# A hybrid encoder layer on one core: GpSimd issues the transfers of the mixer weights' split, only small parts are kept in DRAM, and the last tile is computed by token halves

## The chip, the core and the metric

One core of a Trainium2 chip runs the whole kernel. TensorE (PE) multiplies, VectorE (DVE), ScalarE (ACT) and GpSimd (POOL) do elementwise work, and SyncE (SP) only issues transfers; POOL and ACT can issue them too. Each engine carries out its own instructions in a fixed order and waits at the first one whose inputs or buffers are not ready. The metric is the device time of one launch in microseconds (us).

## The reference

One encoder layer over 512 tokens of width 1024, in float32:

```python
x = x + 0.5 * swiglu(rms_norm(x, ffn1_norm), ffn1_w_gate, ffn1_w_up, ffn1_w_down)   # d_ff 2816
h = rms_norm(x, mix_norm)
proj = h @ w_in
o_a = gdn_mixer(qkv_a, z_a, a_a, b_a, ...)      # gated DeltaNet, 4 heads, two directions, chunks of 64
o_b = dilated_mixer(qkv_b, ...)                 # windowed attention, 8 heads, 3 dilations
x = x + concatenate([o_a, o_b]) @ w_out
x = x + 0.5 * swiglu(rms_norm(x, ffn2_norm), ffn2_w_gate, ffn2_w_up, ffn2_w_down)
x = rms_norm(x, final_norm)
```

## The kernel before

**Layout.** Activations lie with the width on the 128 partitions and all 512 tokens in a row, so x is eight tiles of 128x512. Each float32 product is made from parts: a matrix is split into a big part (hi, a cast to the fp32r format) and a small part (lo, the rest), and `mm3` (line 53 for its matmuls) multiplies hi by hi, hi by lo and lo by hi into one PSUM bank. One weight tile of 8 blocks of 128x128 therefore costs 24 matmuls of 512 columns.

**Stages.** FFN 1: 22 steps f with a gate tile (pg) and an up tile (pu) each, 44 tiles of 24 matmuls, then 8 output tiles (pd) of 66 matmuls. The mixer: projections, attention, DeltaNet and output projection, an order of work written out by hand. FFN 2: as FFN 1, its first gate and up tiles fed as the mixer's are. Then the last norm and the output.

**Weights of the FFNs.** `wload` fetches 512 KB into `wraw` (2 buffers, issued by SP, line 175), ACT casts it to `whi` (line 176), DVE subtracts and writes `wlo` (line 177). TensorE needs both.

**Weights of the mixer.** There are 76 half tiles of 256 KB. During FFN 1 `presplit` prepares them: SP loads `praw` (line 202, 3 buffers), ACT casts it to `phi` (line 205, 2 buffers), DVE subtracts in place (line 206), and `send` has SP store both parts to DRAM (lines 193 and 194, tiles `ws`). `share` deals these steps over FFN 1. In the mixer `wnext` loads both parts again, 512 KB in one transfer (`wsp`, line 216), four tiles of buffers, and no engine but TensorE touches them. The order of the instructions on each engine is fixed when the kernel is built, by a scheduler: where a `phi` stands ahead of a `whi` on ACT, the `whi` can't start before it.

**The norm.** `Norm` squares x on ACT and adds the squares (line 263) on POOL or, with `fast`, on DVE; a matmul with ones (pr) sums over partitions; `rsq` makes the reciprocal root R.

**The end.** The eighth output tile of FFN 2 is computed over all 512 tokens; its two halves are then added to x, squared, summed (pr), turned into R, and all eight output tiles y are multiplied by R on DVE and POOL (line 1237) and stored.

Of the kernel before, what the change touches and what calls it, by code (L numbers as in the profile page):

```python
# [10 lines left out]
F32 = mybir.dt.float32  # L11
# [5 lines left out]
P = 128  # L17
# [16 lines left out]
N_MASK = 768  # L34
LV0, LVG, SCG, ATG = 9.0, 0.625, 0.8, 0.55
GIN, VGO, VGV, PRG, NRG, VTG, VBG, OPG, OTG, FNG, SVG, SSD, SST, VTP, LVH = 9.5, 16.5, 4.0, 0.5, 6.0, 3.5, 3.5, 13.5, 0.75, 10.5, 0.75, 8.0, 0.6, 3.0, 1.3
AHEAD = 3
PRI = 0, 1, 2, 4, 3, 5
ORDER = "rs@1 pa@3 K0 ab gt@2 Q0 K1 bi Q1 pc@3 g0 K3 Q2 K2 g1 Z0 g2 Q3 g3 V0 Pa0 V1 Z3 V2 V3 v0 Pb0 Z2 Z1 Pb1 v1 Pa1 v3 Pa2 Pb2 v2 Pb3 Pa3 oa"

# [50 lines left out]
def encoder_layer(ctx, tc, xT, gu1, dn1, win, wab, wo1, wo2, gu2, dn2, cols, relb, masks, onehot, lnc, sel, out):  # L91
# [49 lines left out]
    ve.tensor_scalar(out=col[:, 0:C_CONV], in0=col[:, 0:C_CONV], scalar1=-0.5, scalar2=None, op0=ALU.mult)  # L141
    gp.memset(ones, 1.0)
    gp.memset(eps, EPS)
    ve.tensor_scalar(out=wqk[:, 0:1], in0=col[:, C_QN:C_QN + 1], scalar1=-0.0625, scalar2=None, op0=ALU.mult)
    ve.tensor_scalar(out=wqk[:, 1:2], in0=col[:, C_KN:C_KN + 1], scalar1=-0.5, scalar2=None, op0=ALU.mult)

# [18 lines left out]
    def wload(src, n, k, low=False, parts=1, then=None):  # L165
        w = n * k
        raw = WF["pool"].tile([P, 1024], F32, tag="raw", name="wraw", bufs=2)
        if low:
            hi, lo = (wp.tile([P, 1024], F32R, tag="w", name=nm, bufs=4) for nm in ("whi", "wlo"))
        else:  # L170
            hi, lo = (WF["pool"].tile([P, 1024], F32R, tag=nm, name=nm, bufs=2) for nm in ("whi", "wlo"))
        sv = src.rearrange("p a b -> p (a b)")
        for i in range(parts):
            s = slice(i * w // parts, (i + 1) * w // parts)
            act["lastf"] = sy.dma_start(out=raw[:, s], in_=sv[:, s])
            se.copy(hi[:, s], raw[:, s])  # L176
            ve.tensor_tensor(out=lo[:, s], in0=raw[:, s], in1=hi.bitcast(F32)[:, s], op=ALU.subtract)  # L177
            if then is not None:
                then(i)
        return (hi[:, :w].rearrange("p (a b) -> p a b", b=k),  # L180
                lo[:, :w].rearrange("p (a b) -> p a b", b=k))
# [3 lines left out]
            for i in range(2)]  # L185
    plan += [wo1[d, :, 4 * u:4 * u + 4] for d in range(4) for u in range(3)] + [wo2[d] for d in range(4)]
    plan += [gu2[0, j, :, 4 * u:4 * u + 4] for j in range(2) for u in range(2)]
    ws_d = [dr.tile([P, 2 * T], F32, name=f"ws{i}") for i in range(len(plan))]
    made, raws, unsent = [0], [], []

    def send():
        i, hi, lo = unsent.pop(0)
        sy.dma_start(out=ws_d[i][:, 0:T], in_=hi.bitcast(F32))
        sy.dma_start(out=ws_d[i][:, T:2 * T], in_=lo)

    def presplit():

        i = made[0]
        made[0] += 1
        for n in range(i if i == 0 else i + 1, min(i + 2, len(plan))):  # L200
            raws.append(tmp("xp", "praw", T + 4, bufs=3)[:, 0:T])
            sy.dma_start(out=raws[-1], in_=plan[n].rearrange("p a b -> p (a b)"))
        lo = raws.pop(0)
        hi = WF["pool"].tile([P, T], F32R, tag="phi", name="phi", bufs=2)
        se.copy(hi, lo)  # L205
        ve.tensor_tensor(out=lo.bitcast(F32R), in0=lo, in1=hi.bitcast(F32), op=ALU.subtract)  # L206
        if unsent:
            send()
        unsent.append((i, hi, lo))

    taken, ready = [0], []

    def wnext():
        while taken[0] < len(plan) and len(ready) <= AHEAD:
            t = wp.tile([P, 1024], F32, tag="w", name="wsp", bufs=4)
            sy.dma_start(out=t, in_=ws_d[taken[0]])
            taken[0] += 1
            ready.append([t[:, i * T:(i + 1) * T].bitcast(F32R).rearrange("p (a b) -> p a b", b=P) for i in range(2)])
        return ready.pop(0)

    def sub(o, a, b):
        ve.tensor_tensor(out=o, in0=a, in1=b.bitcast(F32), op=ALU.subtract)  # L222
# [61 lines left out]
    def ffn(gu, dn, norm, nxt, then=None, late=False, mid=None):  # L284
        with tc.tile_pool(name="wf", bufs=2, reuse_waits="tile") as wf, \
                tc.tile_pool(name="hp", bufs=1, reuse_waits="tile") as hp:
            WF["pool"] = wf
            hh = [hp.tile([P, T], F32R, name=f"hh{f}") for f in range(NF)]
            hl = [hp.tile([P, T], F32R, name=f"hl{f}") for f in range(NF)]
            wait = []  # L290
            for f in range(NF):
                pg, pu = palt("pg"), palt("pu")
                for j, pt in ((0, pg), (1, pu)):
                    if f == 0 and late:
                        for u in (0, 4):
                            wh, wl = wnext()
                            for k in range(u, u + 4):
                                mm3(pt, wh[:, k - u], wl[:, k - u], xh[k], xl[k], k == 0, k == NKT - 1)
                        continue
                    first = then if f == 0 and j == 0 else None  # L300
                    wh, wl = wload(gu[f, j], NKT, P, True, 4 if first else 2 if f == 0 else 1, first)
                    if not late:
                        share(2 * f + j)
                    for k in range(NKT):
                        mm3(pt, wh[:, k], wl[:, k], xh[k], xl[k], k == 0, k == NKT - 1)
                wait.append((f, pg, pu))
                if f == (0 if late else 1):
                    with tc.issue_after(norm.last.ins):
                        for k in range(NKT):
                            norm.sq(k)  # L310
                    norm.rstd()
                if f == 0 and not late:
                    continue
                for e, pg, pu in wait:
                    g, u = tmp("g", "g"), tmp("u", "u")
                    ve.tensor_tensor(out=g, in0=pg, in1=R, op=ALU.mult)
                    silu(g, g)
                    ve.tensor_tensor(out=u, in0=pu, in1=R, op=ALU.mult)
                    ve.tensor_tensor(out=u, in0=u, in1=g, op=ALU.mult)
                    split(hh[e], hl[e], u)  # L320
                wait = []
            for d in range(NKT):
                pd = palt("pd")
                for f0, n in ((0, 8), (8, 8), (16, 6)):
                    wh, wl = wload(dn[d, :, f0:f0 + n], n, P)
                    if not late:
                        share(2 * NF + 3 * d + f0 // 8)
                    for i in range(n):
                        f = f0 + i
                        mm3(pd, wh[:, i], wl[:, i], hh[f], hl[f], f == 0, f == NF - 1)  # L330
                    if late and d == NKT - 1 and f0 == 8:
                        with tc.issue_after(act["mm"].ins):
                            mid()
                for s in (slice(0, 256), slice(256, 512)) if late and d == NKT - 1 else (slice(0, 512),):
                    ve.scalar_tensor_tensor(out=x[d][:, s], in0=pd[:, s], scalar=0.5, in1=x[d][:, s], op0=ALU.mult,
                                            op1=ALU.add)
                nxt(d)

    n1 = Norm(C_F1, 7)

    def bring(i):
        for k in range(1 + 2 * i, min(3 + 2 * i, NKT)):
# [4 lines left out]
    ident = mk[:, M_ID:M_ID + P]  # L347

    vec_d = dr.tile([8, 1024], F32, name="vec_d")
    n2 = Norm(C_MIX, 7)  # L350
    x_d = dr.tile([NKT, P, T], F32, name="x_d")

    def after1(d):
# [6 lines left out]
    with tc.issue_after(act["lastf"].ins):  # L360
        sy.dma_start(out=mk, in_=masks)

    with ExitStack() as mctx:
        mp = mctx.enter_context(tc.tile_pool(name="mp", bufs=1, reuse_waits="tile"))

# [847 lines left out]
            ys.append(slot(f"xh{d}", "y"))  # L1213
            se.mul(ys[d], x[d], col[:, C_FIN + d:C_FIN + d + 1])

    def mid():
        for i, pr in enumerate(prs):
            te.matmul(pr[:, 0:256], lhsT=ones, rhs=n4.acc[:, 256 * i:256 * i + 256], start=True, stop=False)

    ffn(gu2, dn2, n3, last, late=True, mid=mid)  # L1220
    hs = [slice(256 * i, 256 * i + 256) for i in range(2)]
    tail = tmp("sq", "tail")
    preload()
    for pr, s in zip(prs, hs):
        se.activation(tail[:, s], x[7][:, s], AF.Square)
        te.matmul(pr[:, 0:256], lhsT=ones, rhs=tail[:, s], start=False, stop=True)
        rsq(R[:, s], pr[:, 0:256], 1024.0, "u")
    ys.append(slot("xh7", "y"))
    for d in range(NKT):
        y = ys[d]  # L1230
        if d == NKT - 1:
            ve.scalar_tensor_tensor(out=y, in0=x[d], scalar=col[:, C_FIN + d:C_FIN + d + 1], in1=R, op0=ALU.mult,
                                    op1=ALU.mult)
            (sy, se)[d % 2].dma_start(out=out[d], in_=y)
        else:
            for s in hs if d == 0 else (slice(0, T),):
                (gp if d in (1, 4) else ve).tensor_tensor(out=y[:, s], in0=y[:, s], in1=R[:, s], op=ALU.mult)  # L1237
                (sy, se)[d % 2].dma_start(out=out[d, :, s], in_=y[:, s])


def _bucket(rel):
# [77 lines left out]
```

## Time and profile before

| | |
|---|---|
| runs | 1119.83, 1121.74, 1124.93 us; median 1121.74 |
| profiled execution | 1124.95 us, span 1123.2 us |
| FFN 1 gate and up, FFN 1 output | 5.3 to 271.6, 271.6 to 396 us |
| mixer, FFN 2, end | 396 to 746, 746 to 1108, 1108 to 1123.2 us |
| busy share of the span | PE 95%, DVE 55%, ACT 39%, POOL 8% |

The profile comes from one profiled execution. Times in it are in us from the start of the span; the execution's own time is 1.75 us longer than the span. A matmul's recorded duration overlaps the next one's, so its cost is the spacing of starts.

### The profile page before, as it was taken

The page shows a single profiled execution, that of the slowest core. Times are in us where ns is not written, and L with a number is a line of the kernel's source. Part 1 is how long each engine was busy: PE and PEld are TensorE (multiplying, and loading weights), DVE is VectorE, ACT ScalarE, POOL GpSimd, SP SyncE. Part 2 cuts the span into 40 slices and gives each one's busy share as a digit, 9 for nine tenths or more (in the row PEclk, how much of TensorE's full clock was granted, in tenths as well). Part 3 has the DMA queues.
Part 4 walks back from the last instruction along what each step waited for, and adds up shares of the span by engine and source line. Part 5 has one row for each costly group of instructions (what it writes and reads, how often), then busy time and mean ns, then how long its engine had stood idle before and what let it go on. Part 6 is the DMA issues. An engine that isn't in the chain of part 4 may idle for free. (4 is left out here: it accounts for less than half of the span.)

```text
span 1123.2 us, 14359 instructions
## 1 busy us (share of the span) xinstructions
PE 1071.6 (95%) x5312; PEld 871.1 (78%) x5312; DVE 613.1 (55%) x1108; ACT 441.1 (39%) x812; POOL 90.3 (8%) x121
## 2 busy tenths in 40 slices
PE   8999999999999999999999989999999999999994
PEld 5787777777788868778788867778888888888883
DVE  5655655655443358678566778565444444522223
ACT  6533443444332226422574756344332222322221
POOL 3000000000011123440000020100000000001111
PEclk9999999999999999999999999999999999999997
DMA  7788888988993334676723363352222323323332
GB/s 258 263 267 281 278 290 285 297 279 278 305 306 120 99 117 158 188 229 217 181 86 99 112 212 111 110 191 93 95 94 94 97 97 107 96 86 101 100 88 75
DMA packets 85062, 191.99 MB, mean 171 GB/s; under 512 B 21520, under 2 KB 22320, under 8 KB 84992
## 3 DMA queue, kind: packets, MB, share of 16 engines
q1 hardware_dynamic: 80800, 178.68, 49.7%
q0 software_dynamic: 2896, 10.25, 3.0%
q10 hardware_dynamic: 1296, 2.15, 0.5%
q8 instruction: 41, 0.67, 0.3%
q14 instruction: 29, 0.24, 0.1%
HBM read 142.24 MB, written 48.81 MB: 170 GB/s over the span
## 5 line engine op out<-in xcount | busy, mean ns | idle before, releaser
L176 ACT CAST whi<-wraw 128x1024 fp32r<-128x1024 f32 (+1 forms) x138 | 137.5, 998 | 269.0 <-PE pd L53 91.3
L177 DVE TENSOR_TENSOR wlo<-wraw,whi 128x1024 fp32r<-128x1024 f32 (+1 forms) x138 | 159.9, 1159 | 107.4 <-ACT whi L176 105.2
L53 PE MATMUL pg<-xh,whi 128*128 128x512 f32 x344 | 136.8, 398 | 7.2 <-ACT whi L176 7.2
L53 PE MATMUL pg<-xh,wlo 128*128 128x512 f32 x344 | 136.5, 397 | 6.9 <-DVE wlo L177 6.9
L53 PE MATMUL pd<-hh,whi 128*128 128x512 f32 x352 | 137.9, 392 | 2.6 <-ACT whi L176 2.6
L53 PE MATMUL pu<-xh,wlo 128*128 128x512 f32 x344 | 134.8, 392 | 4.8 <-DVE wlo L177 4.8
L53 PE MATMUL pd<-hh,wlo 128*128 128x512 f32 x352 | 137.7, 391 | 0.0
L53 PE MATMUL pd<-hl,whi 128*128 128x512 f32 x352 | 137.5, 391 | 0.0
L53 PE MATMUL pg<-xl,whi 128*128 128x512 f32 x344 | 135.9, 395 | 0.1
L53 PE MATMUL pu<-xh,whi 128*128 128x512 f32 x344 | 134.1, 390 | 0.0
L53 PE MATMUL pu<-xl,whi 128*128 128x512 f32 x344 | 133.9, 389 | 0.0
L206 DVE TENSOR_TENSOR praw<-praw,phi 128x512 fp32r<-128x512 f32 x76 | 53.4, 706 | 116.1 <-ACT phi L205 116.0
L205 ACT CAST phi<-praw 128x512 fp32r<-128x512 f32 x76 | 47.0, 620 | 155.7 <-DMA praw<-in_win 103.3
L53 PEld LDWEIGHTS pg<-xh,wlo 128*128 128x128 f32 x344 | 65.3, 190 | 24.8 <-DVE wlo L177 11.3
L53 PEld LDWEIGHTS pg<-xh,whi 128*128 128x128 f32 x344 | 65.3, 190 | 22.5 <-ACT whi L176 8.7
L53 PEld LDWEIGHTS pu<-xh,wlo 128*128 128x128 f32 x344 | 64.5, 188 | 21.5 <-DVE wlo L177 8.4
L53 PEld LDWEIGHTS pd<-hh,whi 128*128 128x128 f32 x352 | 66.5, 189 | 16.7 <-ACT whi L176 3.1
L53 PEld LDWEIGHTS pd<-hh,wlo 128*128 128x128 f32 x352 | 66.3, 188 | 14.7 <-DVE wlo L177 0.9
L53 PEld LDWEIGHTS pg<-xl,whi 128*128 128x128 f32 x344 | 65.1, 189 | 16.1 <-DVE xl L269 2.5
L53 PEld LDWEIGHTS pd<-hl,whi 128*128 128x128 f32 x352 | 66.5, 189 | 14.0
L53 PEld LDWEIGHTS pu<-xl,whi 128*128 128x128 f32 x344 | 64.6, 188 | 13.5
L53 PEld LDWEIGHTS pu<-xh,whi 128*128 128x128 f32 x344 | 64.6, 188 | 13.5 <-ACT whi L176 0.3
(292 smaller groups left out, 1626.9 us busy)
## 6 DMA issues: line engine op xcount, KB each, us to landing
wraw<-in_gu SPq DMA_DIRECT2D x84, 512.0 KB, 3.9
wsp<-ws SPq DMA_DIRECT2D x76, 512.0 KB, 3.5
ws<-phi SPq DMA_DIRECT2D x76, 256.0 KB, 3.6
ws<-praw SPq DMA_DIRECT2D x76, 256.0 KB, 4.5
wraw<-in_dn SPq DMA_DIRECT2D x32, 512.0 KB, 3.6
praw<-in_win SPq DMA_DIRECT2D x56, 256.0 KB, 4.2
wraw<-in_dn SPq DMA_DIRECT2D x16, 384.0 KB, 3.2
praw<-in_wo SPq DMA_DIRECT2D x16, 256.0 KB, 4.1
```

What stands on the lines that cost most here:

```text
L53: self.last = f(*a, **k)
L176: se.copy(hi[:, s], raw[:, s])
L177: ve.tensor_tensor(out=lo[:, s], in0=raw[:, s], in1=hi.bitcast(F32)[:, s], op=ALU.subtract)
L205: se.copy(hi, lo)
L206: ve.tensor_tensor(out=lo.bitcast(F32R), in0=lo, in1=hi.bitcast(F32), op=ALU.subtract)
```

## The change

Four edits. First, POOL issues the loads and the stores of `presplit`, with four buffers of `praw` and loads two half tiles ahead; only the small part is stored. In the mixer, SP loads the small part (256 KB) and the raw weight (256 KB, into `wrw`, a tile cut in two halves), and ACT casts the big part from it (`wsp<-wrw`); three tiles of buffers hold hi and lo, the fourth is `wrw`. Second, the norms of FFN 1 and of the mixer add their squares on DVE. Third, the last output tile is computed for tokens 0 to 255 and then for 256 to 511, and the norm, the products with R and the stores of the first half are placed after the first matmuls of the second. Fourth, eight matmuls of ones by ones stand at the start.

```diff
+    pw = pat("warm")
+    for i in range(8):
+        te.matmul(pw[:, 0:P], lhsT=ones, rhs=ones, start=True, stop=True)
...
-            hi, lo = (wp.tile([P, 1024], F32R, tag="w", name=nm, bufs=4) for nm in ("whi", "wlo"))
+            hi, lo = (wtile(nm) for nm in ("whi", "wlo"))
...
     def send():
-        i, hi, lo = unsent.pop(0)
-        sy.dma_start(out=ws_d[i][:, 0:T], in_=hi.bitcast(F32))
-        sy.dma_start(out=ws_d[i][:, T:2 * T], in_=lo)
+        i, lo = unsent.pop(0)
+        gp.dma_start(out=ws_d[i], in_=lo)
     def presplit():
         i = made[0]
         made[0] += 1
-        for n in range(i if i == 0 else i + 1, min(i + 2, len(plan))):
-            raws.append(tmp("xp", "praw", T + 4, bufs=3)[:, 0:T])
-            sy.dma_start(out=raws[-1], in_=plan[n].rearrange("p a b -> p (a b)"))
+        if unsent:
+            send()
+        for n in range(0 if i == 0 else i + 2, min(i + 3, len(plan))):
+            raws.append(tmp("xp", "praw", T + 4, bufs=3)[:, 0:T] if n % 4 else
+                        WF["pool"].tile([P, T], F32, tag="praw", name="praw", bufs=1))
+            gp.dma_start(out=raws[-1], in_=plan[n].rearrange("p a b -> p (a b)"))
         lo = raws.pop(0)
-        hi = WF["pool"].tile([P, T], F32R, tag="phi", name="phi", bufs=2)
+        hi = WF["pool"].tile([P, T], F32R, tag="phi", name="phi", bufs=1)
         se.copy(hi, lo)
         ve.tensor_tensor(out=lo.bitcast(F32R), in0=lo, in1=hi.bitcast(F32), op=ALU.subtract)
-        if unsent:
-            send()
-        unsent.append((i, hi, lo))
-
-    taken, ready = [0], []
+        unsent.append((i, lo))
...
+    def wtile(name, dt=F32R):
+        nw[0] += 1
+        t, n = ("wb", 1) if nw[0] % 4 == 0 else ("wa", 3)
+        return wp.tile([P, 1024], dt, tag=t, name=name, bufs=n)
+    def fetch(i):
+        if i < len(plan):
+            r = wraw[0][:, i % 2 * T:(i % 2 + 1) * T]
+            sy.dma_start(out=r, in_=plan[i].rearrange("p a b -> p (a b)"))
+            fetched.append(r)
+    def wopen():
+        while nw[0] % 4 != 3:
+            nw[0] += 1
+        wraw.append(wtile("wrw", F32))
+        for i in range(2):
+            fetch(i)
     def wnext():
-        while taken[0] < len(plan) and len(ready) <= AHEAD:
-            t = wp.tile([P, 1024], F32, tag="w", name="wsp", bufs=4)
-            sy.dma_start(out=t, in_=ws_d[taken[0]])
-            taken[0] += 1
-            ready.append([t[:, i * T:(i + 1) * T].bitcast(F32R).rearrange("p (a b) -> p a b", b=P) for i in range(2)])
-        return ready.pop(0)
+        while got[0] < len(plan) and len(ready) < 3:
+            t = wp.tile([P, 1024], F32R, tag="wa", name="wsp", bufs=3)
+            sy.dma_start(out=t[:, T:2 * T].bitcast(F32), in_=ws_d[got[0]])
+            ready.append(t)
+            got[0] += 1
+        while got[1] < got[0] - (got[0] < len(plan)):
+            i = got[1] - got[0] + len(ready)
+            se.copy(ready[i][:, 0:T], fetched.pop(0))
+            got[1] += 1
+            fetch(got[1] + 1)
+        t = ready.pop(0)
+        return [t[:, i * T:(i + 1) * T].rearrange("p (a b) -> p a b", b=P) for i in range(2)]
...
+            if late:
+                d = NKT - 1
+                ws = [wload(dn[d, :, f0:f0 + n], n, P, f0 == 0) for f0, n in ((0, 8), (8, 8), (16, 6))]
+                for i in range(2):
+                    pd, s = palt("pd"), slice(256 * i, 256 * i + 256)
+                    for f in range(NF):
+                        wh, wl = ws[f // 8]
+                        mm3(pd[:, 0:256], wh[:, f % 8], wl[:, f % 8], hh[f][:, s], hl[f][:, s], f == 0, f == NF - 1)
+                        if (i, f) in ((0, 15), (1, 4)):
+                            with tc.issue_after(act["mm"].ins):
+                                mid(i)
+                    ve.scalar_tensor_tensor(out=x[d][:, s], in0=pd[:, 0:256], scalar=0.5, in1=x[d][:, s], op0=ALU.mult,
                                             op1=ALU.add)
...
-    n1 = Norm(C_F1, 7)
+    n1 = Norm(C_F1, 7, True)
...
-    n2 = Norm(C_MIX, 7)
+    n2 = Norm(C_MIX, 7, True)
...
+    wopen()
...
+    def close(i):
+        s, pr = hs[i], prs[i]
+        te.matmul(pr[:, 0:256], lhsT=ones, rhs=n4.tail[:, s], start=False, stop=True)
+        rsq(R[:, s], pr[:, 0:256], 1024.0, "u")
+        for d in range(NKT):
+            y = ys[d]
+            if d == NKT - 1:
+                ve.scalar_tensor_tensor(out=y[:, s], in0=x[d][:, s], scalar=col[:, C_FIN + d:C_FIN + d + 1], in1=R[:, s],
+                                        op0=ALU.mult, op1=ALU.mult)
+            else:
+                (gp if d in (1, 4) else ve).tensor_tensor(out=y[:, s], in0=y[:, s], in1=R[:, s], op=ALU.mult)
+            (se if i and d % 2 else sy).dma_start(out=out[d, :, s], in_=y[:, s])
+    def mid(i):
+        if i == 0:
+            for pr, s in zip(prs, hs):
+                te.matmul(pr[:, 0:256], lhsT=ones, rhs=n4.acc[:, s], start=True, stop=False)
+            ys.append(slot("xh7", "y"))
+            n4.tail = tmp("sq", "tail")
+            preload()
+        else:
+            se.activation(n4.tail[:, hs[0]], x[7][:, hs[0]], AF.Square)
+            close(0)
...
+    se.activation(n4.tail[:, hs[1]], x[7][:, hs[1]], AF.Square)
+    close(1)
```

**The start, on DVE.** The rows run from the second split of x (`xl`) to the first work after it; `wlo` of 128x256 is a quarter of the first gate tile, `praw<-praw,phi` is the subtraction for a mixer half tile. Before:

```order
L269 SCALAR_TENSOR_TENSOR xl_237<-x_73,col,xh_236 128x512
L269 SCALAR_TENSOR_TENSOR xl_242<-x_74,col,xh_241 128x512
L177 TENSOR_TENSOR wlo<-wraw,whi 128x256
L269 SCALAR_TENSOR_TENSOR xl_250<-x_75,col,xh_249 128x512
L269 SCALAR_TENSOR_TENSOR xl_255<-x_76,col,xh_254 128x512
L177 TENSOR_TENSOR wlo<-wraw,whi 128x256
L269 SCALAR_TENSOR_TENSOR xl_263<-x_77,col,xh_262 128x512
L269 SCALAR_TENSOR_TENSOR xl_268<-x_78,col,xh_267 128x512
L177 TENSOR_TENSOR wlo<-wraw,whi 128x256
L269 SCALAR_TENSOR_TENSOR xl_276<-x_79,col,xh_275 128x512
```

Now:

```order
L298 SCALAR_TENSOR_TENSOR xl_246<-x_73,col,xh_245 128x512
L298 SCALAR_TENSOR_TENSOR xl_251<-x_74,col,xh_250 128x512
L179 TENSOR_TENSOR wlo<-wraw,whi 128x256
L211 TENSOR_TENSOR praw<-praw,phi 128x512
L298 SCALAR_TENSOR_TENSOR xl_259<-x_75,col,xh_258 128x512
L298 SCALAR_TENSOR_TENSOR xl_264<-x_76,col,xh_263 128x512
L179 TENSOR_TENSOR wlo<-wraw,whi 128x256
L211 TENSOR_TENSOR praw<-praw,phi 128x512
L298 SCALAR_TENSOR_TENSOR xl_272<-x_77,col,xh_271 128x512
L298 SCALAR_TENSOR_TENSOR xl_277<-x_78,col,xh_276 128x512
L179 TENSOR_TENSOR wlo<-wraw,whi 128x256
L211 TENSOR_TENSOR praw<-praw,phi 128x512
```

Three subtractions for mixer half tiles have moved in among the splits of x, one after each pair of tiles; before, none came until all eight tiles of x were split.

**Gate and up of FFN 1.** On the queues, before: SP held the loads of FFN weights and all transfers of the mixer half tiles in one order:

```order
L175 DMA wraw<-in_gu 128x1024
L202 DMA praw<-in_win 128x512 x2
L193 DMA ws_111<-phi 128x512
L194 DMA ws_111<-praw 128x512
L193 DMA ws_112<-phi 128x512
L175 DMA wraw<-in_gu 128x1024
L202 DMA praw<-in_win 128x512
L194 DMA ws_112<-praw 128x512
L193 DMA ws_113<-phi 128x512
L194 DMA ws_113<-praw 128x512
L193 DMA ws_114<-phi 128x512
```

Now POOL holds the latter (SP keeps only the loads of `wraw` here), in its order:

```order
L195 DMA ws_124<-praw 128x512
L207 DMA praw<-in_win 128x512
L195 DMA ws_125<-praw 128x512
L207 DMA praw<-in_win 128x512 x2
L195 DMA ws_126<-praw 128x512
L195 DMA ws_127<-praw 128x512
L207 DMA praw<-in_win 128x512
L195 DMA ws_128<-praw 128x512
L207 DMA praw<-in_win 128x512
L195 DMA ws_129<-praw 128x512
```

The store of the big part (`ws<-phi`) is gone, and loads and stores of the mixer half tiles take turns on POOL.

In the same stretch on ACT, where `g` and `hh` belong to the FFN's activation, before:

```order
L205 CAST phi<-praw 128x512
L176 CAST whi<-wraw 128x1024
L151 ACTIVATE g<-g 128x512
L205 CAST phi<-praw 128x512
L176 CAST whi<-wraw 128x1024
L205 CAST phi<-praw 128x512
L225 CAST hh_188<-u 128x512
L205 CAST phi<-praw 128x512
L176 CAST whi<-wraw 128x1024
```

Now:

```order
L210 CAST phi<-praw 128x512 x2
L178 CAST whi<-wraw 128x1024
L153 ACTIVATE g<-g 128x512
L210 CAST phi<-praw 128x512 x2
L178 CAST whi<-wraw 128x1024
L210 CAST phi<-praw 128x512
L254 CAST hh_196<-u 128x512
L210 CAST phi<-praw 128x512 x2
L178 CAST whi<-wraw 128x1024
L153 ACTIVATE g<-g 128x512
```

Counted over the whole order, three `phi` stand to each two `whi` before. Now five do, from the eleventh `whi` (14 `phi` ahead of it) to the thirty-seventh, ahead of which all 76 stand; behind that one none is left.

**The mixer, on SP.** `D<-M` is a small transfer of the DeltaNet's, which comes in four bursts of eight; what an instruction waits for stands behind it (`PE` frees a buffer, `Activation` is ACT's cast, the `DMA` names are landings). Before:

```order
L216 DMA wsp<-ws_105 128x1024 [waits DMAHW6_49,PE_49]
L216 DMA wsp<-ws_106 128x1024 [waits DMAHW7_49,PE_49]
L216 DMA wsp<-ws_107 128x1024 [waits DMAHW0_49,PE_49]
L216 DMA wsp<-ws_108 128x1024 [waits DMAHW1_49,PE_49]
L216 DMA wsp<-ws_109 128x1024 [waits DMAHW2_49,PE_49]
L640 DMA D_3160<-M 32x4x32 [waits DVE_49,Activation_49]
L640 DMA D_3160<-M 32x4x32 x2
```

Now:

```order
L239 DMA wsp<-ws_115 128x512 [waits DMAHW0_49,DMASW6_49,PE_49]
L225 DMA wrw<-in_win 128x512 [waits DMAHW3_49,Activation_49]
L239 DMA wsp<-ws_116 128x512 [waits DMAHW2_49,DMASW0_49,PE_49]
L225 DMA wrw<-in_win 128x512 [waits DMAHW5_49,Activation_49]
L239 DMA wsp<-ws_117 128x512 [waits DMAHW4_49,DMASW1_49,PE_49]
L225 DMA wrw<-in_win 128x512 [waits DMAHW7_49,Activation_49]
L679 DMA D_3096<-M 32x4x32 [waits DVE_49]
L679 DMA D_3096<-M 32x4x32
L679 DMA D_3096<-M 32x4x32 [waits DMAHW6_49]
L679 DMA D_3096<-M 32x4x32 [waits DVE_49]
```

Each load of 512 KB that waited for PE alone has become a load that waits for PE and a load that waits for ACT, in turns in one queue; the burst of `D<-M` stands among them as before.

## Rows read from the trace of the kernel before

**Rows 1.** Windows: busy us and count of each engine, PE clock, DMA share, GB/s.

```profile
60.00:271.60 211.60, 200.28 (x860) 159.35 (x859) 120.32 (x160) 85.56 (x124) 0.72 (x1) 1.00 0.87 282
...
308.00:396.00 88.00, 88.00 (x390) 72.82 (x389) 35.92 (x34) 26.09 (x35) 11.86 (x17) 1.00 0.52 169
396.00:746.00 350.00, 334.09 (x2131) 273.59 (x2130) 248.12 (x657) 165.06 (x433) 54.04 (x84) 1.00 0.49 155
746.00:1108.00 362.00, 362.00 (x1593) 298.45 (x1591) 149.26 (x175) 112.03 (x141) 10.17 (x6) 1.00 0.31 95
```

**Rows 2.** Timeline of PE at three places: start, duration, what, idle before.

```profile
5.32 0.80 PE L53 MATMUL pg<-xh,whi 128*128 128x512 f32 x1 [5.32 <-ACT whi L176]
...
14.17 0.39 PE L53 MATMUL pu<-xh,whi 128*128 128x512 f32 x1
...
43.01 0.39 PE L53 MATMUL pu<-xh,wlo 128*128 128x512 f32 x1
...
50.41 0.40 PE L53 MATMUL pg<-xh,whi 128*128 128x512 f32 x1
...
286.37 0.39 PE L53 MATMUL pd<-hh,wlo 128*128 128x512 f32 x1
289.38 0.79 PE L53 MATMUL pd<-hh,whi 128*128 128x512 f32 x1 [2.63 <-ACT whi L176]
...
292.84 0.40 PE L53 MATMUL pd<-hl,whi 128*128 128x512 f32 x1
```

**Rows 3.** Waits in 60 to 271.6 us: total us, times, longest.

```profile
ACT phi L205 <- DMA praw<-in_win: 94.5, 31, 5.9
...
SPq L202 <- DMA ws<-praw: 44.8, 28, 3.6
```

**Rows 4.** Groups by line, 60 to 271.6 us: busy us, mean ns, idle before.

```profile
L176 ACT CAST whi<-wraw 128x1024 fp32r<-128x1024 f32 x36 | 37.6, 1045 | 3.9 <-DMA wraw<-in_dn 3.8
L206 DVE TENSOR_TENSOR praw<-praw,phi 128x512 fp32r<-128x512 f32 x53 | 36.4, 690 | 78.3 <-ACT phi L205 78.3
L205 ACT CAST phi<-praw 128x512 fp32r<-128x512 f32 x53 | 32.9, 620 | 113.8 <-DMA praw<-in_win 94.5 <-DMA praw<-in_wo 11.0 <-DMA ws<-phi 8.4
```

**Rows 5.** DMA issues, 60 to 280 us: count, size, median us to landing.

```profile
ws<-praw SPq DMA_DIRECT2D x54, 256.0 KB, 4.8
praw<-in_win SPq DMA_DIRECT2D x44, 256.0 KB, 4.5
```

**Rows 6.** Windows: the stretch with the most DMA traffic, columns as in rows 1.

```profile
280.00:308.00 28.00, 25.33 (x104) 19.94 (x103) 12.45 (x16) 10.75 (x16) 0.00 (x0) 0.94 0.96 310
```

**Rows 7.** DMA issues, 396 to 560 us.

```profile
wsp<-ws SPq DMA_DIRECT2D x44, 512.0 KB, 4.3
int_d<-itr POOLq DMA_DIRECT2D x8, 256.0 KB, 2.9
```

**Rows 8.** Timeline of DVE at the start.

```profile
9.24 1.44 DVE L269 SCALAR_TENSOR_TENSOR xl<-x,col,xh 128x512 fp32r<-128x512 f32 x2
```

**Rows 9.** Timeline of SP in the mixer.

```profile
451.28 4.69 SPq L640 DMA_DIRECT2D D<-M  x8
```

**Rows 10.** Timeline of PE: eight matmuls of 256 columns and the next.

```profile
570.87 1.21 PE L51 MATMUL pov<-PT,vb 128*128 128x256 f32 x8
572.01 0.27 PE L51 MATMUL pl<-M,tts 64*64 64x64 f32 x1
```

**Rows 11.** The end: group, timeline of DVE, DMA issues.

```profile
L335 DVE SCALAR_TENSOR_TENSOR x<-pd,x 128x256 f32<-128x256 f32 x2 | 0.8, 420 | 8.8 <-PE pd L53 8.8
...
1112.96 5.29 DVE L1237 TENSOR_TENSOR y<-y,R 128x256 f32<-128x256 f32 x6
...
1118.18 0.74 DVE L1232 SCALAR_TENSOR_TENSOR y<-x,col,R 128x512 f32<-128x512 f32 x1
...
out_y<-y SPq DMA_DIRECT2D x3, 256.0 KB, 2.4
out_y<-y SPq DMA_DIRECT2D x2, 128.0 KB, 1.9
```

More of the change, by code (lines that the diff above doesn't have):

```diff
@@ L36 @@
 GIN, VGO, VGV, PRG, NRG, VTG, VBG, OPG, OTG, FNG, SVG, SSD, SST, VTP, LVH = 9.5, 16.5, 4.0, 0.5, 6.0, 3.5, 3.5, 13.5, 0.75, 10.5, 0.75, 8.0, 0.6, 3.0, 1.3
-AHEAD = 3
 PRI = 0, 1, 2, 4, 3, 5
@@ L187, in encoder_layer @@
     plan += [gu2[0, j, :, 4 * u:4 * u + 4] for j in range(2) for u in range(2)]
-    ws_d = [dr.tile([P, 2 * T], F32, name=f"ws{i}") for i in range(len(plan))]
+    ws_d = [dr.tile([P, T], F32, name=f"ws{i}") for i in range(len(plan))]
     made, raws, unsent = [0], [], []
     def send():
-        i, hi, lo = unsent.pop(0)
-        sy.dma_start(out=ws_d[i][:, 0:T], in_=hi.bitcast(F32))
-        sy.dma_start(out=ws_d[i][:, T:2 * T], in_=lo)
+        i, lo = unsent.pop(0)
+        gp.dma_start(out=ws_d[i], in_=lo)
     def presplit():
@@ new lines, in encoder_layer @@
+    nw, got, fetched, ready, wraw = [0], [0, 0], [], [], []
+    def wtile(name, dt=F32R):
[13 more added lines that the diff above has]
+            fetch(i)
@@ L321, in ffn @@
                 wait = []
-            for d in range(NKT):
+            for d in range(NKT - 1 if late else NKT):
                 pd = palt("pd")
@@ L330, in ffn @@
                         mm3(pd, wh[:, i], wl[:, i], hh[f], hl[f], f == 0, f == NF - 1)
[L331 to L335, printed above, removed]
+                ve.scalar_tensor_tensor(out=x[d], in0=pd, scalar=0.5, in1=x[d], op0=ALU.mult, op1=ALU.add)
+                nxt(d)
+            if late:
[10 more added lines that the diff above has]
+                    ve.scalar_tensor_tensor(out=x[d][:, s], in0=pd[:, 0:256], scalar=0.5, in1=x[d][:, s], op0=ALU.mult,
                                             op1=ALU.add)
                 nxt(d)
-    n1 = Norm(C_F1, 7)
+    n1 = Norm(C_F1, 7, True)
     def bring(i):
@@ L1214, in last @@
             se.mul(ys[d], x[d], col[:, C_FIN + d:C_FIN + d + 1])
-    def mid():
-        for i, pr in enumerate(prs):
-            te.matmul(pr[:, 0:256], lhsT=ones, rhs=n4.acc[:, 256 * i:256 * i + 256], start=True, stop=False)
-    ffn(gu2, dn2, n3, last, late=True, mid=mid)
[L1221 to L1238, printed above, removed]
+    hs = [slice(256 * i, 256 * i + 256) for i in range(2)]
```

## The prediction

> **What bounds the kernel now.** I read the windows by stage first. From 746 to 1108 us PE is busy the whole time: 362.00 us for 1593 matmuls, 0.2272 us each, and 308 to 396 us is as full [rows 1]. So FFN 2 and the second half of FFN 1's output tiles can't be shortened except by fewer columns. FFN 1 is the same work (1056 matmuls of gate and up, 528 of output: 1584 x 0.2272 = 359.9 us) but takes from the first matmul at 5.32 to 396.0, 390.7 us. It loses 30.8 us, all before 308.
>
> The timeline of PE says where [rows 2]. The first 24 matmuls take 5.32 to 14.17, 8.85 us for 5.45 us of work: 3.4 lost. At the norm, 13 starts from 43.01 to 50.41 take 7.40 for 2.95: 4.5 lost. At the start of the output tiles, 8 starts from 286.37 to 292.84 take 6.47 for 1.82: 4.65 lost, and the row names ACT's `whi`. The other 18.3 us are spread over gate and up.
>
> What ACT waits for there is the table of waits: 94.5 us, 31 times, for a load of `praw`; and SP waits 44.8 us for the store of a small part, which must land before its buffer can be loaded again [rows 3]. Behind such a `phi` stands a `whi`. 36 `whi` and 53 `phi` lie in 211.6 us [rows 4], so a pair of tiles takes 11.76 us where its 48 matmuls need 10.91. A pair carries 2 x 512 KB plus 3 x 768 KB (load, two stores), 3.41 MB; the DMA's share is 0.87 at 282 GB/s [rows 1]. Both a ring of three buffers and the DMA's rate explain the loss: with landings of 4.5 and 4.8 us [rows 5] plus cast 0.62 and subtraction 0.69 a buffer turns in 10.6 us before any queueing, and three presplits in 11.76 us is one turn.
>
> **The change, part by part** (against the profiled execution's own 1124.95 us, 0.3% above the median of 1121.74).
>
> *Presplit in gate and up.* Thirteen pairs of tiles now carry five presplits each (62 of them), then none is left. Bytes per pair: 2 x 512 KB + 5 x 512 KB = 3.67 MB, in 10.91 us 336 GB/s. The fullest stretch of the trace moves 310 GB/s at a share of 0.96 [rows 6]. At 310 a pair takes 11.84 us, 0.93 lost, 12 us over thirteen; at 282, the rate of this stretch now, 13.01, 27 us. The new ring is four buffers: a turn is two landings, cast and subtraction, and two issues on POOL (about 0.7 each, bounded by POOL's one DMA in this stretch at 0.72 busy [rows 1]). With the landings of rows 5 that is 12.0 us, 3.0 per presplit; with 2.9 us each, what POOL's 256 KB transfers take in the mixer [rows 7], 8.5, so 2.13. The engines need 10.91/5 = 2.18. I take 294 GB/s, between the two rates, since one store in three is gone and a fourth buffer keeps more in flight: 12.48 us a pair, 1.58 x 13 = 20.5 us lost, in place of 18.3: **+2.2** (from -18 to +27, the ring at 3.0: 62 x 3.0 = 186 against 141.8, 44 lost, so up to +26).
>
> The Trainium skill ("DMA: Bandwidth & Descriptors", section "Issuing engines are not separate DMA queues") says that transfers issued by several engines interleave on the same 16 engines, and that issuing from more engines saves only the time of issuing. By that rule POOL's queue alone gives nothing, the rate stays at 282 GB/s, and this term is +9 in place of +2.2; the first sentence of the second rival below says so in rows. No run here shows two engines issuing at once in this stretch, so the trace neither bears it out nor speaks against it.
>
> *The output tiles of FFN 1.* All presplits are done by then, so the stop at 286.37 goes: **-4.65** (0 if another wait takes its place).
>
> *The norm.* The order has four `phi` and the R chain ahead of the same `whi`; squares are added on DVE, at 0.69 us each by the nearest row [rows 4], 14 of them, covered by DVE's idle time (120 of 211.6 busy, 36 of 88 in the output tiles [rows 1]). The stop stays: **0** (-4 to +4).
>
> *The start.* DVE runs splits of x without a gap there, two in 1.44 us [rows 8], and three subtractions of 0.69 now stand among them: 2.07. ACT gets three casts of 0.62 beside them. Four loads of 256 KB, 1 MB, compete with x: 3.4 us at 310 GB/s. Most of that lies beside the splits: **+4** (1.8 to 5.5). The eight matmuls of ones run before 5.32, while PE waits for the first cast: 0.
>
> *The mixer.* 76 casts of 0.62, 47 us, raise ACT from 165 to 212 of 350 us [rows 1]. Each tile needs two transfers of 256 KB through SP instead of one of 512 KB; same bytes. With three tiles of buffers a load issued when a tile is freed has two tiles' work to land, 24 x 0.2272 = 5.5 us in a dense run, where it had 8.2. It landed in 4.3 us at 512 KB [rows 7], so 256 KB alone fits, but a burst of `D<-M` ahead of it holds SP for 4.69 [rows 9]: 4.3 + 4.7 = 9.0, short by 3.5, where before it was short by 0.8. That is 2.7 more at each of the four bursts, 11 at most; several fall where other work is at hand: **+3** (0 to +11). The raw half in `wrw` returns every second tile, 5.5 us, for landing, 0.62 of cast and 0.32 of issue, so it holds while landing stays below 4.5 us.
>
> *The end.* Eight products with R, from 1112.96 to 1118.92, 6.0 us [rows 11], become those of one half: six on DVE at 0.42 (the row of 256-column operations), 2.5 us, the first half's lying beneath PE's matmuls: -3.4. The norm's chain loses a staggered second half, -0.4, and the last transfer is 128 KB, 1.9 us in place of 2.4: -0.5. PE pays: eight matmuls of 256 columns take 570.87 to 572.01 [rows 10], at most 0.1425 each, and half a column count is 0.1136; 132 of them are 15.0 to 18.8 us in place of 15.0. I take 0.3 for it, since a group of eight ends with its own tail: **-4** (-5 to 0).
>
> Sum: 2.2 - 4.65 + 0 + 4 + 3 - 4 = +0.55, so 1125.5 on the profiled execution's scale and **1122.3** on the median's.
>
> **The rivals** (all on the median's scale).
>
> *Faster: the queues keep pace.* If POOL's ring turns in 2.13 us per presplit, `phi` never waits and gate and up lose nothing: 1122.3 - 20.5 = 1102; at 310 GB/s 8.4 less, 1114. For it: the window of rows 6 shows the DMA can, and SP no longer waits for `praw` in front of `wraw`. Against: 336 GB/s is above anything in the windows. It decides at a turn of 8.7 us. About 1107.
>
> *Slower: rate or ring hold ACT.* If the rate stays at 282 GB/s, 27 us are lost in place of 20.5: 1129. If landings stay at 4.5 and 4.8 us under the denser demand, a presplit takes 2.75 to 3.0 us, and `phi` blocks `whi`: 29 to 44 us lost in place of 20.5, so 1131 to 1146, about 1138. For it: the landings of rows 5 were measured at 282 GB/s, less than is now asked. Against: with one store fewer per presplit there is less in flight. It decides above 2.5 us per presplit.
>
> *Slower: the mixer's two loads.* If raw halves land later than 4.5 us, or ACT reaches a cast late behind its other work, some 0.2 us for each of the 76 tiles adds 15 where I have 3: 1134. For it: two chains in one queue, each waiting for another engine. Against: 350 us hold 76 x 12 x 0.2272 = 207 us of these tiles' matmuls, so other work is at hand.
>
> *No effect:* gate and up are bound by DMA either way, and start and mixer eat what the end and the output tiles give. That is my sum.
>
> **Chances and range.** The sum, 1116 to 1128: 0.36. Queues keep pace: 0.29. Rate or ring: 0.20. Mixer: 0.13. A mishap at start or end: 0.02. Half a per cent, 5.6 us, is what a measurement can tell from no change. Faster 0.29, same 0.36, slower 0.35. Leaving out about a third of the first and of the second rival's reach (below 1106, above 1140) gives 1106 to 1140.
>
> **What would show it.** In gate and up: windows near 294 GB/s with a share over 0.9 up to about the 37th `whi`, waits of ACT for `praw` still in the table, then PE full to 396 without a stop. At the start: the first `pu` some 4 us later. In the mixer: PE waiting on `wsp` for a few us, behind the bursts of `D<-M`. At the end: about 11 us after the last matmul instead of 15. Wrong would be my rate (12.48 us a pair) or the lead in the mixer, before anything else.

## The result, and the profile after

The changed kernel takes 1170.67 us (median of four runs, 1162.58 to 1174.41) where before takes 1123.34 beside it: 1.041 times as long, interval 1.0344 to 1.0477. The forecast was 1122.3 in a range of 1106 to 1140, so the time lies outside it; of the rivals, "rate or ring hold ACT" went the right way and not far enough. The profiled execution has a span of 1169.1 us, 45.9 more than before.

The windows of the changed kernel by stage (us, busy us and count of PE, PEld, DVE, ACT, POOL, PE's clock, DMA share, GB/s); they answer to [rows 1]:

```profile
60.00:240.00 180.00, 148.49 (x574) 112.30 (x573) 95.31 (x128) 69.69 (x105) 61.77 (x115) 0.93 0.71 233
240.00:316.50 76.50, 76.33 (x333) 62.68 (x332) 38.11 (x46) 26.86 (x34) 3.67 (x13) 0.99 0.43 139
316.50:436.20 119.70, 119.70 (x529) 99.08 (x528) 40.09 (x46) 32.37 (x42) 1.80 (x5) 1.00 0.38 115
436.20:791.90 355.70, 334.08 (x2129) 273.38 (x2129) 247.79 (x657) 204.50 (x504) 53.91 (x84) 1.00 0.51 152
791.90:1155.40 363.50, 363.42 (x1661) 302.43 (x1660) 153.87 (x185) 115.00 (x147) 11.57 (x8) 1.00 0.31 96
```

From the timeline: where the first up tile begins, and the fourteenth and the last cast of a mixer half tile on ACT, as in [rows 2]:

```profile
17.31 0.40 PE L52 MATMUL pu<-xh,whi 128*128 128x512 f32 x1
...
49.78 0.62 ACT L210 CAST phi<-praw 128x512 fp32r<-128x512 f32 x1 [0.99 <-DMA praw<-in_win]
...
248.42 0.62 ACT L210 CAST phi<-praw 128x512 fp32r<-128x512 f32 x1 [1.97 <-DMA praw<-in_gu]
```

Waits of 60 to 240 us (total, times, longest), the answer to [rows 3], and landings of the same stretch, the answer to [rows 5]:

```profile
POOL praw L207 <- DMA ws<-praw: 107.1, 36, 5.0
...
ACT phi L210 <- DMA praw<-in_win: 66.6, 27, 5.7
...
PE pg L52 <- ACT whi L178: 12.3, 8, 2.4
```

```profile
ws<-praw POOLq DMA_DIRECT2D x58, 256.0 KB, 4.4
...
praw<-in_win POOLq DMA_DIRECT2D x38, 256.0 KB, 4.4
```

By stage, after less before: the start +3.1 (17.31 against 14.17), the rest of gate and up +41.8 (to 316.5 instead of 271.6), the output tiles of FFN 1 -4.8 (119.7 instead of 124.5), the mixer +5.9 (355.7 instead of 349.8), FFN 2 with the end -0.1. Nearly the whole loss is in the stretch where the `phi` stand packed: 62 of them in 248.42 - 49.78 = 198.6 us, 3.20 us each. The 26 weight tiles among them need 26 x 5.45 = 141.7 us of TensorE, which allows 2.29; 57 us are lost there. While that goes on PE has 148 of 180 us busy at a clock of 0.93, and the DMA engines move 233 GB/s at a share of 0.71, less than before. After the last `phi` PE is full to the end of FFN 1. POOL stands 107 us in 36 waits of one kind: a load of `praw` for the store that frees its buffer.

Followed buffer by buffer through the trace (means over 58 presplits), a turn, from one load into a buffer to the next, is 12.8 us: the load lands in 4.3, the cast starts 0.6 later, the subtraction 1.0 after that, the store is issued 2.0 after the subtraction's start and lands in 4.5, and the next load is issued 0.5 later. With four buffers that is the 3.2 us of a presplit. So the DMA engines are not full; the buffers come round too late for the order.

### The profile page after: what moved, and what is told of

Same layout as the page of the kernel before. It is cut to its first block, busy times and chain, and to the rows that moved or that the text cites. A ratio compares the mean times of both kernels' runs of the same rounds, so it can differ in the third digit from the quotient of the medians.

```text
span 1169.1 us, 14704 instructions
## 1 busy us (share of the span) xinstructions
PE 1090.9 (93%) x5394; PEld 886.1 (76%) x5394; DVE 616.0 (53%) x1125; ACT 483.8 (41%) x888; POOL 152.4 (13%) x263
## 4 chain that ended last, share of the span: by engine, by line
PE 66%; DMA 13%; DVE 7%; issue 7%; POOL 3%; ACT 3%; SPq 0%; DVEq 0%; POOLq 0%; ACTq 0%
PE pd L52 21%; PE pg L52 14%; PE pu L52 14%; DMA ws<-praw 8%; PE pc L50 4%; PE pd L50 2%; PE pqk L50 2%; POOL praw L207 2%; DMA praw<-in_win 2%; PE ps L50 2%; PE pl L50 1%; PE pvb L50 1%; PE pz L50 1%; PE pT L50 1%; DMA rdb<-rd_d 1%
## 5 line engine op out<-in xcount | busy, mean ns | idle before, releaser
L52 PE MATMUL pg<-xh,whi 128*128 128x512 f32 x344 | 140.8, 409 | 18.9 <-ACT whi L178 13.0
L52 PE MATMUL pu<-xh,whi 128*128 128x512 f32 x344 | 136.9, 398 | 10.4 <-ACT whi L178 10.4
L52 PE MATMUL pg<-xh,wlo 128*128 128x512 f32 x344 | 139.4, 405 | 4.1 <-DVE wlo L179 4.1
L52 PE MATMUL pd<-hh,whi 128*128 128x512 f32 (+1 forms) x374 | 141.2, 378 | 0.0
L52 PE MATMUL pd<-hh,wlo 128*128 128x512 f32 (+1 forms) x374 | 140.9, 377 | 0.0
L52 PE MATMUL pd<-hl,whi 128*128 128x512 f32 (+1 forms) x374 | 140.8, 377 | 0.0
L52 PEld LDWEIGHTS pd<-hl,whi 128*128 128x128 f32 x374 | 70.3, 188 | 13.1
L52 PEld LDWEIGHTS pd<-hh,whi 128*128 128x128 f32 x374 | 70.3, 188 | 12.9
L52 PEld LDWEIGHTS pd<-hh,wlo 128*128 128x128 f32 x374 | 70.3, 188 | 12.8
L347 DVE TENSOR_TENSOR u<-pu,R 128x512 f32<-128x512 f32 x44 | 30.3, 688 | 87.7 <-PE pu L52 87.7
```

Source lines behind the costliest of these rows:

```text
L52: self.last = f(*a, **k)
```

## The experiments

Ratios are to the kernel before, run beside each group of experiments (medians 1123.82, 1125.33 and 1125.75 us). Rows and stage times come from one profiled execution each; in e3, e5 and e6 it was the longest of the ten (1141.15, 1129.06 and 1129.57 us), so their losses by stage are rather too large.

**e1: the casts spread.** Each `phi` is put behind the newest `whi`:

```diff
-            se.copy(hi[:, s], raw[:, s])
+            act["whi"] = se.copy(hi[:, s], raw[:, s])
...
-        se.copy(hi, lo)
+        with tc.issue_after(act["whi"].ins):
+            se.copy(hi, lo)
```

> The changed kernel with one edit: the cast of each mixer half tile may not stand ahead of the newest cast of an FFN weight tile on ScalarE, so that 76 presplits are dealt over 60 weight tiles (about 1.27 to a tile) instead of 62 over 26. Ring theory (a presplit takes a quarter of a turn of four buffers, 3.2 us in the changed kernel's trace): a tile of 5.45 us then needs 1.27 x 3.2 = 4.1 us, so gate and up lose nothing to it and the stage falls from 311 to some 250 us: about 1170 - 60 = 1110 us. Rate theory (the DMA engines can't move more than the 234 GB/s of that stretch while GpSimd issues): 1.19 MB a tile in 5.45 us is 218 GB/s, so nearly the same, 1110 to 1120. Rival (casts ahead of the weight casts are not what holds TensorE, but GpSimd's issuing): no change, 1165 to 1175.

1107.76 us, 0.9844 of before (0.9812 to 0.9876). Window and landings of that kernel:

```profile
60.00:240.00 180.00, 180.00 (x796) 149.12 (x795) 109.97 (x143) 76.34 (x108) 45.04 (x84) 1.00 0.66 218
...
wraw<-in_gu SPq DMA_DIRECT2D x33, 512.0 KB, 3.5
praw<-in_win POOLq DMA_DIRECT2D x42, 256.0 KB, 4.2
ws<-praw POOLq DMA_DIRECT2D x42, 256.0 KB, 4.2
```

PE is busy for the whole 180 us and does 796 matmuls in it instead of 574; the last `phi` comes at 350 us instead of 248. Nothing else was changed, so in this kernel the packing in the order cost 63 us. That is as much as the 45 that the change lost and the 18 that gate and up lost before; whether packing was the cause of the 18 too is the question of e6. The rival falls. POOL's landings are hardly shorter at 218 GB/s (4.2 us) than in the packed order (4.4); they have 4.3 us a presplit now, and that is enough.

**e2: three buffers instead of four.**

```diff
-            raws.append(tmp("xp", "praw", T + 4, bufs=3)[:, 0:T] if n % 4 else
-                        WF["pool"].tile([P, T], F32, tag="praw", name="praw", bufs=1))
+            raws.append(tmp("xp", "praw", T + 4, bufs=3)[:, 0:T])
```

> The changed kernel with three buffers for the raw mixer half tiles instead of four; the order on ScalarE packs slightly less (54 casts over 25 weight tiles). Ring theory: a presplit takes a third of the same 12.8 us turn, 4.3 us, so about 64 x 4.3 = 273 us instead of 198, less four more weight tiles that lie in the stretch: some 50 us longer, 1220 us. Rate theory: the pace of 3.2 us is set by the DMA engines, so the time stays within 5 us of 1170.

1176.28 us (two runs), 5.6 more than the changed kernel; the simple ring expected 50 more. Between the fourteenth and the last `phi` (56.01 and 277.70 us) a presplit takes 3.58 us, so a turn of three is 10.7 us, where a turn of four is 12.8. Its landings:

```profile
ws<-praw POOLq DMA_DIRECT2D x51, 256.0 KB, 3.7
...
praw<-in_win POOLq DMA_DIRECT2D x40, 256.0 KB, 3.9
```

With less in flight the transfers land sooner, 3.7 instead of 4.4 us for the store. A turn is no constant, and a buffer more is worth 0.4 us a presplit, not 1.1. The 62 presplits take 23 us longer, but four more weight tiles lie among them, 22 us of TensorE's work, so the time hardly moves. That speaks against both theories as I had written them: neither a fixed turn nor a fixed rate.

**e3: SyncE issues the presplit's transfers** (`gp` replaced by `sy` in both places, four buffers, the casts packed).

> The changed kernel with SyncE instead of GpSimd issuing the presplit's loads and stores; four buffers, only small parts stored, two ahead. Ring theory: the turn is two landings, cast, subtraction and two issues, 0.33 instead of 0.54 each, so 12.4 instead of 12.8 us and 3.1 a presplit; the weight loads now stand behind the waits for stores in the same queue. Between 1160 and 1175. Theory that GpSimd's transfers are slow in themselves: landings fall from 4.2 to about 3.5 us, a turn to 11 us: about 1140. Beside it, the end: GpSimd's last DRAIN lasts 7.1 us beyond its last product in the changed kernel and 3.4 before; if it grows with the transfers that GpSimd issued, it goes back to 3.4 here and the span behind the last matmul falls from 14.1 to 11 us; if it doesn't, it stays at 14.

1132.14 us, 1.0065 of before (1.0034 to 1.0096), 38.5 less than the changed kernel and 28 below the ring theory's range. Window, landing and GpSimd's last instruction:

```profile
60.00:240.00 180.00, 159.20 (x645) 122.76 (x644) 107.10 (x143) 79.21 (x117) 0.26 (x4) 0.96 0.80 259
...
ws<-praw SPq DMA_DIRECT2D x62, 256.0 KB, 4.6
...
L1360 POOLq DRAIN  x3: 46/98/5211, 1132.9 to 1139.1; - x3
```

A presplit takes 2.89 us (55.16 to 234.61 us for 62), a turn 11.6, with landings of 4.6 us. SyncE's landings are not shorter at all, so the theory of slow transfers falls; the turn is shorter, and gate and up with the start take 280.2 us instead of 311.2. From the start of a subtraction to the issue of its store it is 2.0 us in the changed kernel and 0.9 here (means over 56 and 58 presplits of the traces): on POOL the store stands behind a load that waits for an older store. In the trace of the changed kernel the transfer just ahead of a store in its queue was issued only after the subtraction had ended in 38 of 58 presplits, here in 7 of 58. I read the difference as that queue's order; no run changed the order alone, so this part is argued. The first up matmul is back at 13.5 us, and the end gains what was expected: the DRAIN, GpSimd's last long instruction, lasts 5.2 us instead of 9.0, and 10.8 us lie behind the last matmul.

**e4: the old end.** The last tile and the last norm as before.

> The changed kernel with the last output tile and the last norm as before (all 512 tokens at once). Theory (the end's gain is eaten by GpSimd's last DRAIN): the last product on GpSimd ends 8.3 us behind the last matmul and the DRAIN takes 7 more, so the span ends 15 to 16 us behind the last matmul instead of 14.1, and the whole is at most 2 us slower than the changed kernel. Rival (the halves gain their 4 us and something else in FFN 2 takes them): 4 us slower, the end at 18 us behind the last matmul.

1172.83 us, 2.2 more than the changed kernel. Behind the last matmul lie 16.2 us: GpSimd's last product ends 8.3 us behind it, and the span ends 7.9 after that. So the DRAIN sets the end with either form of it. By this reading the rival of a full 4 us, which wanted 18, falls; the runs (1168.52 to 1174.55 us) overlap with those of the changed kernel and could not tell 2 us from 4.

**e5: spread, and SyncE issues.**

> The spread order of the first experiment, and SyncE issuing the presplit's transfers as in the third. Theory that GpSimd's transfers carry a longer landing of their own: in the first experiment 256 KB of GpSimd's landed in 4.2 us while 512 KB of SyncE's landed in 3.5 in the same stretch, so SyncE's 256 KB should land in about 3 us here. Rival (landing follows the load alone): 4.2 us stays. For the time: gate and up stay full under either; the start gets its 3.9 us back (first up matmul at 13.5 instead of 17.4, because GpSimd's four early loads no longer compete with x) and the end 3.3 us (the DRAIN): 1107.8 - 7 = about 1100.5 us. If SyncE's weight loads get stuck behind its waits for stores, 5 to 10 us more.

1124.87 us, 0.9994 of before (0.9976 to 1.0012): 24 more than expected and 17 more than e1 with POOL issuing. The expectation had named weight loads stuck behind waits for stores, but at 5 to 10 us. The waits of 60 to 240 us, of ACT and of SP's queue:

```profile
ACT whi L178 <- DMA wraw<-in_gu: 72.6, 20, 6.9
...
SPq L207 <- DMA ws<-praw: 130.9, 34, 7.0
```

SP waits 131 us for stores before it may load `praw` again, and the loads of FFN weights stand behind in the same queue; ACT waits 73 us for them. In the output tiles it is worse: 260.10 to 395.81 us, 135.7 instead of 119.7. Start and end gained as expected (13.3 us to the first up matmul, 10.8 behind the last). On the landings: loads took 3.4 us, stores 4.9, against 4.2 and 4.2 from POOL in e1, so no clear word on which engine's transfers are slower.

**e6: the kernel before with the spread casts alone.**

> The kernel before with the spread order alone: hi and lo both stored, three buffers, SyncE issuing. Theory that the packing of the order was the loss: 1.27 presplits to a tile need 1.27 x 3.95 = 5.0 us of the 5.45, so the 18 us of gate and up go, and the stop at the first output tile as well unless presplits that now reach into the output tiles make another: 1124 - 20 = 1104 us. Rate theory (282 GB/s is what the engines give): a tile now asks 1.52 MB in 5.45 us, 279 GB/s, at the edge; in the output tiles 293 GB/s, so a few us are lost there: 1110 us. If both parts' storing is the loss: no change, 1119 or more.

1128.35 us, 1.0012 (0.9986 to 1.0037): no change, expected was 20 less. The same waits:

```profile
ACT whi L176 <- DMA wraw<-in_gu: 54.6, 24, 4.1
...
SPq L202 <- DMA ws<-praw: 94.0, 38, 5.2
```

From the first up matmul, gate and up take 251.7 us instead of 257.4, where e1 takes 235.7; the output tiles, into which presplits now reach, take 132.6 instead of 124.5. So the packing alone explains about a quarter of what gate and up lost before, and the output tiles lose more than that. There too the weight loads stand behind the waits for stores, and spreading the casts mostly moves the wait from `phi` to `whi`.

**e7: the kernel before with the new end alone.**

> The kernel before with the last output tile and norm by token halves alone. Theory: GpSimd issued only 40 transfers, its DRAIN lasts 3.4 us beyond its last product, which is hidden beneath the last outputs, so the end gains what the forecast said: 10.8 us behind the last matmul instead of 15.6, less 1.4 us more of matmuls: 3.4 us faster, about 1120.4. Rival (the halves' gain is lost whoever issues): no change.

1120.76 us, 0.9959 (0.9944 to 0.9973), 4.6 less than before. Behind the last matmul lie 10.8 us instead of 15.6. With 1.4 us more of matmuls the halves are worth 3.4 us in the trace, near the forecast's 4, where GpSimd has issued few transfers.

**e8: e1, with the last half's two GpSimd products on VectorE.**

```diff
-                (gp if d in (1, 4) else ve).tensor_tensor(...)
+                (gp if d in (1, 4) and i == 0 else ve).tensor_tensor(...)
```

> The first experiment with the last half's two products of GpSimd moved to VectorE, so that GpSimd's last product is that of the first half, some 8 us earlier. DRAIN theory (it begins when GpSimd's last product ends and lasts some 7 us because GpSimd issued 192 transfers): it ends before the outputs have landed, the end falls from 14.1 to about 11.5 us behind the last matmul (VectorE pays 0.9), 1105 us. Rival (the DRAIN waits for something at the very end): no gain, 1108.

1103.67 us, 0.9803 (0.9774 to 0.9832), 4.1 less than e1; 10.4 us behind the last matmul instead of 14.1. The DRAIN is as long as in e1 (8.9 us), but it begins at 1084.7, ahead of the last matmul at 1088.1:

```profile
L1361 POOLq DRAIN  x3: 46/98/8897, 1084.7 to 1098.2; - x3
```

**e9: e8, with GpSimd's first four loads held until the last tile of x has landed.**

```diff
+            if n < 4:
+                gp.tensor_tensor(out=raws[-1][:, 0:1], in0=x[7][:, 0:1], in1=x[7][:, 0:1], op=ALU.add)
             gp.dma_start(out=raws[-1], in_=plan[n].rearrange("p a b -> p (a b)"))
```

> The eighth experiment, and GpSimd's first four loads made to wait until the last tile of x has landed (each buffer's first column is first written by GpSimd from that tile). Theory that these loads' traffic beside x is what the start lost: the first up matmul goes from 17.1 to about 13.5 us and the time from 1103.7 to about 1100. Rival (the start is late because GpSimd holds something else, or because of the ones matmuls): the first up matmul stays at 17.

1101.37 us, 0.9782 (0.9754 to 0.981), the lowest median of the study, though its runs overlap with those of e8. The first up matmul begins at 13.42 instead of 17.10. The landing of x before, in the changed kernel and here (0 to 20 us):

```profile
x<-in_xT SPq DMA_DIRECT2D x8, 256.0 KB, 5.4
```

```profile
x<-in_xT SPq DMA_DIRECT2D x8, 256.0 KB, 7.7
```

```profile
x<-in_xT SPq DMA_DIRECT2D x8, 256.0 KB, 4.8
```

**e10: both parts stored, spread, POOL issuing, the end of e8.** It is the kernel before with these edits: three transfers a presplit on POOL, three buffers, and a mixer that loads both parts.

> The kernel before with the spread order, GpSimd issuing the presplit's loads and both stores, the new end with the last products on VectorE; hi and lo both stored, three buffers, and the mixer loading both parts as before. It tells what dropping the big part is worth. Theory that a queue of its own and the spread order are the whole gain: a tile asks 1.52 MB in 5.45 us, 279 GB/s, which SyncE's queue alone moved before, and the ring of three turns in 12 us, 4.0 a presplit of the 4.28 there are; gate and up lose nothing and the mixer takes 350 us instead of 355: about 1099. Rival (without the big part's 20 MB less the queues don't keep up, or three GpSimd transfers a presplit turn slower than 12.9 us): 10 to 40 us lost in FFN 1, 1110 to 1140.

1174.24 us, 1.0424 (1.039 to 1.0459). The rival's side, and worse than its price:

```profile
POOL praw L202 <- DMA ws<-praw: 120.7, 27, 7.5
ACT phi L206 <- DMA ws<-phi: 76.8, 20, 6.6
```

With three transfers a presplit on POOL the two buffers of `phi` and the three of `praw` both come back too late; a presplit takes 5.4 us (89.35 to 422.48 us for 62) where 4.3 are to be had. With SyncE issuing and both parts stored (e6) it took 4.65. So spreading and a queue of its own are not enough while both parts are stored; e10 also has a buffer of `praw` less than e8, and no run separates the two, but the wait for `ws<-phi` exists only where the big part is stored. The mixer takes 349.0 us here, against 354.7 in e9 and 349.8 before: loading a part and casting the other costs the mixer 5 to 6 us (the eight profiles with the new mixer lie at 352.4 to 360.3 us, the four with the old one at 347.2 to 352.7).

## Why the prediction was wrong

**Gate and up, the step that failed.** "I take 294 GB/s, between the two rates", 12.48 us a pair of tiles: the thirteen pairs took 198.6 us, 15.3 each, and the term, +2.2, measured +41.8. The step that failed was to price the pace of the presplits by the rate that the DMA engines can reach. They moved 233 GB/s at a share of 0.71, under the 0.96 of [rows 6], so they were not the limit. The limit was the ring of buffers: four buffers, a turn of 12.8 us, 3.20 us a presplit. The ring's own sum, from [rows 5], stood in the same paragraph at 12.0 us, 3.0 a presplit and "up to +26"; it was the better one, and its landings and issues were about right, but it had no time for a store that stands behind a late load on POOL, 1.3 us between the subtraction's end and the store's issue. At 3.20 the 62 presplits lose 57 us in place of 18.3, +38.5; the rest of the 41.8 is not split further.

The packing of the order was in the sum, five presplits to a pair, and that a `phi` holds up a `whi` was in the second rival. The runs show that it takes both: the order asks for a presplit every 2.29 us and the ring gives one every 3.20. e1 leaves buffers and queues as they are, asks for one in 4.3 us, and the whole loss is gone; e3 leaves the packing, the ring gives one in 2.89, and much of the loss is gone.

**The norm**: 0 forecast, and the stop stayed; it is part of the 41.8:

```profile
53.85 0.79 PE L52 MATMUL pg<-xh,whi 128*128 128x512 f32 x1 [4.28 <-DVE u L348]
```

In e1 it is gone: 1032 matmuls x 0.2272 = 234.5 us, and gate and up take 235.7 from the first up matmul. The squares added on DVE were never run alone.

**A second queue.** The Trainium skill ("DMA: Bandwidth & Descriptors", section "Issuing engines are not separate DMA queues") says that issuing from several engines only saves the time of issuing. Between e1 and e5 only the issuer differs, and POOL is 17 us faster although start and end favour SyncE by some 7. The measurement decides: what a second queue saves here is waiting, since a weight load no longer stands behind a load that waits for a store. It is no gain by itself: with the casts packed POOL is 38.5 us slower than SyncE (the changed kernel against e3).

**The output tiles**: -4.65 forecast, -4.8 measured; the stop is gone.

**The start**: +4 forecast, +3.1 measured, but for the wrong half of the reason. In e1 no subtraction stands among the splits, and the first up matmul still begins at 17.4; in e9 the loads wait and it begins at 13.4. It was the traffic of the four early loads: x landed in 7.7 us with them beside it and in 4.8 where they wait (5.4 before). The three subtractions were covered.

**The mixer**: +3 in 0 to +11 forecast, +5.9 measured, but mostly not by the forecast's mechanism. TensorE's idle time there rises from 15.4 to 21.1 us. Loads of mixer weights end 2.7 us of it, where they ended 0.6 before; VectorE ends 14.1, where it ended 9.3. The waits for such loads, before and after:

```profile
PE pc L51 <- DMA wsp<-ws: 0.6, 2, 0.3
```

```profile
PE pc L50 <- DMA wsp<-ws: 1.6, 1, 1.6
PE pz L50 <- DMA wsp<-ws: 1.1, 1, 1.1
```

So it was in part luck that the term lay in its range; why the results of VectorE come later stays open.

**The end**: -4 forecast; -4.8 in e7, less 1.4 for the matmuls of 256 columns, which I had at 0.3 (FFN 2 takes 363.1 instead of 361.7 us to its last matmul). In the changed kernel it came to -0.1, because of an instruction that I hadn't read: GpSimd's DRAIN at the end of the program. The last semaphores of all engines come only after it, from 1168.4 on. In the changed kernel (shortest, median and longest in ns, first and last start):

```profile
L1360 POOLq DRAIN  x3: 46/98/8972, 1159.3 to 1168.8; - x3
```

The long one begins at 1159.3, so it ends at 1168.3, 7.1 us after GpSimd's last product (1161.2), 3.3 us after SyncE's last wait for the outputs was over (1165.0). Before:

```profile
L1314 POOLq DRAIN  x3: 46/93/6061, 1113.2 to 1122.8; - x3
```

It ended at 1119.3 there, 3.4 us after the last product, beneath the outputs.

**The ones matmuls** moved nothing that the profile shows: the first matmul of the FFN begins at 5.30 instead of 5.32. No run left them out alone.

## What to carry to other kernels

Where buffers go round through two transfers, add up a whole turn, with its landings, its casts and the time that a store stands behind other transfers in its queue; divide it by the buffers, and compare that with what the order asks per tile. A DMA share well under 1 does not mean that the loop keeps pace. In these kernels, background work packed ahead of the work on the path made every late transfer a stall: put the background work behind the newest step of the path, and give its waits a queue in which nothing urgent stands. Both are needed: spread alone (e5, e6) and a queue of its own alone (the changed kernel) gained nothing, together 16 us (e1). And the loop must still keep pace: with both parts stored and three buffers (e10) spread and queue together lost 48 us.

## What the hardware showed that I had not expected

GpSimd's DRAIN at the end of the program differed between kernels in which GpSimd had issued different numbers of transfers, but it did not simply grow with the number. It lasted 3.4 us beyond its last product with 40 of them (before, e3, e5, e6, e7), 7.1 with 192 (the changed kernel, e1, e2, e4, e8, e9), and 4.7 with 268 (e10, where it ends at 1164.8 and the last product at 1160.15):

```profile
L1331 POOLq DRAIN  x3: 46/93/6442, 1158.4 to 1171.6; - x3
```

So the number of transfers alone does not set it, and what does stays open. Ending GpSimd's work some microseconds earlier hides it (e8).
